# GDN's memory on the right, RWKV's first operands beside GDN's last scan, and a second place for inverses

## The chip, the cores and the metric

The kernel runs on one core of a Trainium2 chip. The metric is the device time of one execution in microseconds. Three runs of the kernel before gave 3955.95, 3957.01 and 3962.45 us.

## What is computed

Two blocks follow each other on 1024 tokens of width 1024, in float32. The first has two layers; each does this:

```python
h = rms_norm(x, norm_g[layer])
cols = split_columns(h @ w_in[layer])
y_gdn = gdn_branch(cols, ...)    # gated delta rule, 6 heads, both directions, chunks of 64
y_mla = mla_branch(cols, ...)    # attention, 6 heads, low-rank q and kv, rope
y_rwkv = rwkv7_branch(cols, ...) # RWKV-7 recurrence, 4 heads, both directions
mix = concat([y_gdn, y_mla, y_rwkv]) * silu(cols['gate'])
x = x + mix @ w_out[layer]
```

The second block (a gated convolution and a gated linear recurrence) is not touched by the change. It fills the span from about 2500 us on.

## The kernel before

**Stages of a layer.** `layer` (L1664) runs stage A, the projection `h @ w_in` together with the GDN branch, then stage B, MLA together with RWKV, and then the product with `w_out`. All matmuls with weights are split into high and low parts: `product` (L1039) sends three matmuls for every 128 rows of the sum, each recorded at L1045, 48 for one tile of 128 output columns. The projection has 27 such tiles, in the order of `ORDER`; `job` (L1690) stores each half tile to `proj` in DRAM, and whoever needs it loads it from there. The last eight tiles are the gate.

**GDN.** Heads go in three pairs. `gdn_front` (L217) prepares a pair in five parts between its `yield`s: convolutions of q and k; convolution of v, transposes and the decay matrix; the products within a chunk; an inverse on VectorE (`lane_inverse`, L462) and the loads of q2; and the rest of the inverse with the products that the scan needs. `gdn_scan` (L411) is a chain of 14 steps: eight small matmuls into a PSUM tile `psk` (L440), then an addition on VectorE (L442), on which the next step waits. Among the steps it makes the outputs in `pso` (L428, L430); after them come additions (L447), a norm on ScalarE and a last scaling (L458).

**RWKV.** `rwkv_prep` (L501) and `rwkv_features` (L532) load projected tiles and shift them along the tokens (`load_shifted`, L490: a load into a tile `pad`, then L485 to L487). Units 0 to 3 are two groups of heads in two directions. For each, `rwkv_early` (L547) makes the operands `kb` and `rk` (L572 to L599), then `ga` and `gb` from their products, transposes a part of `ga` into `lan` (L635), and inverts it on POOL with `lane_inverse` into `xl` (L468 on ScalarE, then 60 instructions at L475 and L476). `rwkv_late` (L642) turns `xl` (L690, L692) and makes what the scan needs; `rwkv_scan` (L747) is again a chain of 14 steps.

**MLA.** `mla` (L854) loads its three projected tiles on POOL's queue (L864 to L867), norms them, and goes through 24 blocks of scores, softmax and values; it yields at every matmul.

**What sets the order.** The text of the program gives each instruction its precedence. The planner that lays out the program walks through a simulated time and gives an engine, whenever it is free, the ready instruction that was written first; on the chip every engine then follows that order. Two strings set what is written when:

```python
SEQ_A = "0 T6 0 1 1 T6 1 0 S0 1 1 2 2 2 T5 S1 2 2 S2"
SEQ_B = "F0 V0 E0 E1 F1 L0 S0+L12 V1 S1+E22 E3 L2 S2+L32 O0 S3 O1"
```

In SEQ_A a number is the next part of that pair's `gdn_front`, S is its scan, and T6 writes six tiles of the projection. Four tiles stand ahead of the string, and what is left (six tiles here) is written after it. `paced` (L1091) ties every third matmul of the projection to a no-op on SP's queue, so that other work can get in between. In SEQ_B each word is a part of RWKV (F features, V values, E early, L late, S scan, O finish), and `weave` (L782) writes eight steps of MLA ahead of every step of RWKV.

**Memory.** Pools are stacked from the left end of SBUF or, with `side="right"`, from the right; a tile waits for the tiles whose place it takes. On the left lie, in stage A, the normed input `hh` and `hl` with the projection's weights, and above them GDN's tiles; in stage B RWKV's pools `r` and `s` and MLA's `m` take their places. PSUM has eight banks. Stage A uses pss 1 (scan steps), pso 1 (scan outputs), ps 3 (fronts) and psd 2 (projection); stage B uses mT 2, mS 2, rx 3 and mo 1. RWKV's `xl` and `lan` have one buffer each (`RWKV_BUFS`).

Of the kernel before, what the change touches and what calls it, by code (L numbers as in the profile page):

```python
# [95 lines left out]
class K:  # L96
# [19 lines left out]
    def psum(self, ex, **banks):  # L116

        return [
            ex.enter_context(self.tc.tile_pool(name=self.name(nm), bufs=b, space=PSUM, reuse_waits="tile"))
            for nm, b in banks.items()  # L120
        ]
# [289 lines left out]
def gdn_scan(k, hp, F, prm, y_out):  # L411
# [23 lines left out]
    for s in range(1, NST - 1):  # L435
        psk = k.pss.tile([128, 512], F32, tag="sc", name=n("psk"))
# [12 lines left out]
    for x, sl in zip(y, HALVES):  # L449
        sq = F["free"][1][:, sl]  # L450
        nc.scalar.activation(sq, x, AF.Square)
        ps = k.pss.tile([128, 512], F32, tag="sc", name=n("ps"))
# [9 lines left out]
def lane_inverse(k, eng, pool, lan):  # L462
# [3 lines left out]
    xt = pool.tile([128, 32, 32], F32, tag="xl", name=k.name("xl"))  # L466
# [80 lines left out]
def rwkv_early(k, gi, d, F, prm, P, w2a2, E):  # L547
# [12 lines left out]
    lan = g.tile([64, 32, 32], F32, tag="lan", name=n("lan"))  # L560
# [47 lines left out]


# [6 lines left out]
    for b in range(4):  # L616
# [7 lines left out]
        for z, ps in enumerate(pss):  # L624
# [4 lines left out]
            yield  # L629
    for q in range(2):  # L630
# [8 lines left out]
    E.update(kb=kb, rk=rk, ga=ga, gb=gb, ep=ep, xl=lane_inverse(k, nc.gpsimd, g, lan))  # L639
# [1024 lines left out]
def layer(k, L, xs, x_in, x_out, prm_d, prm_at, w_in, w_out, wuq, wukv, cs, next_g):  # L1664
# [3 lines left out]
    with ExitStack() as lx:  # L1668
# [11 lines left out]
        with ExitStack() as hx:  # L1680
            k.pss, k.pso, k.ps, k.psd = k.psum(hx, pss=1, pso=1, ps=3, psd=2)
            hp_ = hx.enter_context(tc.tile_pool(name=n("h"), bufs=1, reuse_waits="tile"))
            hh = hp_.tile([128, 8, T], F32R, name=n("hh"))
            hl = hp_.tile([128, 8, T], F32R, name=n("hl"))
            xs.split_norm(pf("ng"), lambda i, sl: (hh[:, i, sl], hl[:, i, sl]))
            xs.close()
            with ExitStack() as gx:
                wpool = gx.enter_context(tc.tile_pool(name=n("w"), bufs=1, reuse_waits="tile"))
                k.wp = Tagged(wpool, dict(wr=2, wh=3, wl=3, st=2))

                def job(i):
                    def evac(hf, sl, ps):
                        st = k.wp.tile([128, 512], F32, tag="st", name=n("st"))[:, : sl.stop - sl.start]
                        nc.scalar.activation(st, ps, AF.Silu if i >= TI["gate"] else AF.Copy)
                        nc.scalar.dma_start(proj[i][:, sl], st)
                    return w_in[i], ((lambda j: hh[:, j]), (lambda j: hl[:, j])), evac

                steps = dense_steps(k, map(job, ORDER), wait=True)

                tiles = lambda n: run(itertools.islice(steps, n * 48))  # L1700
                tiles(4)
                steps = paced(k, steps)
                with tc.tile_pool(name=n("g"), bufs=1, reuse_waits="tile") as g:
                    k.g = Tagged(g, GDN_BUFS)
                    decays = []
                    fronts = [gdn_front(k, hp, [proj[1 + 3 * hp + a] for a in range(3)], pf, decays, eg) for hp in range(3)]
                    next(fronts[0])
                    misc, _ = pair_of(k, "misc")
                    nc.sync.dma_start(misc, proj[0])
                    decays.extend(gdn_prep(k, misc, pf, eg))  # L1710
                    next(fronts[0])
                    F = [None] * 3
                    for x in SEQ_A.split():
                        if x[0] == "T":
                            tiles(int(x[1:]))
                        elif x[0] == "S":
                            gdn_scan(k, int(x[1]), F[int(x[1])], pf, ys[int(x[1])])
                        else:
                            F[int(x)] = next(fronts[int(x)])
                    run(steps)  # L1720
        with ExitStack() as px:
            k.mT, k.mS, k.rx, k.mo = k.psum(px, mT=2, mS=2, rx=3, mo=1)

            rp, r2, mp = (px.enter_context(tc.tile_pool(name=n(x), bufs=1, reuse_waits="tile")) for x in ("r", "s", "m"))
            k.g = Tagged(rp, RWKV_BUFS, {x: r2 for x in ("ga", "gb", "vz", "lan", "xl", "lt")})
            k.rm = reset_mask(k, rp, T, 0, CH)
            k.constants(rp, "rw", "rwf", "rwb")
            P = rwkv_prep(k, proj[TI["wdad"]], pf)
            w2a2 = rp.tile([128, 2, 256], F32, name=n("w2a2"))
            nc.sync.dma_start(w2a2.rearrange("p d c -> p (d c)"), prm_d[:, npr:])  # L1730
            steps = mla(k, mp, [proj[0], proj[TI["cq0"]], proj[TI["ckv"]]], pf, wuq, wukv, cs, ys[3:6])
            Fs, Es, yts = {}, {}, {}

            def part(x):
                w, u = x[0], int(x[1])
                gi, d = u // 2, u % 2
                if w == "F":
# [117 lines left out]
```

## Time and profile before

| | |
|---|---|
| median of three runs | 3957.01 us |
| the profiled execution's own time | 3981.41 us |
| its span, first to last instruction | 3979.6 us |
| mean granted TensorE clock | 0.916 |
| TensorE busy | 3454.4 us (87%) |
| VectorE, ScalarE, POOL busy | 59%, 45%, 35% |

Times in the rows are microseconds from the span's start. Engines are PE (TensorE), PEld (its weight loads), DVE (VectorE), ACT (ScalarE), POOL and SP; a q behind a name is the engine's queue. A row of a window gives its borders and its length, then the busy time of PE, PEld, DVE, ACT and POOL with the count of instructions (PE alone where one line is asked for), then the granted clock as a share of full speed, the busy share of the DMA engines and GB/s. A row of a timeline gives start, duration, engine, line, operation, what is written and read, and in brackets the engine's idle time ahead of it with what ended it. A row of a group gives its count, its busy time, the mean of one in ns and the idle time ahead of it. Idle time is a window's length less the busy time.

In layer 0 the third GDN scan runs from 560 to 610 us, the projection ends at about 640, MLA's first instruction is at 610, and stage B ends at about 1200. Layer 1 repeats this some 1280 to 1290 us later.

### The profile page before, as it was taken

The page shows a single profiled execution, that of the slowest core. Times are in us where ns is not written, and L with a number is a line of the kernel's source. Part 1 is how long each engine was busy: PE and PEld are TensorE (multiplying, and loading weights), DVE is VectorE, ACT ScalarE, POOL GpSimd, SP SyncE. Part 2 cuts the span into 40 slices and gives each one's busy share as a digit, 9 for nine tenths or more (in the row PEclk, how much of TensorE's full clock was granted, in tenths as well). Part 3 has the DMA queues.
Part 4 walks back from the last instruction along what each step waited for, and adds up shares of the span by engine and source line. Part 5 has one row for each costly group of instructions (what it writes and reads, how often), then busy time and mean ns, then how long its engine had stood idle before and what let it go on. Part 6 is the DMA issues. An engine that isn't in the chain of part 4 may idle for free. (4 is left out here: it accounts for less than half of the span.)

```text
span 3979.6 us, 72088 instructions
## 1 busy us (share of the span) xinstructions
PE 3454.4 (87%) x30444; PEld 2710.6 (68%) x30444; DVE 2349.3 (59%) x3138; ACT 1780.1 (45%) x2798; POOL 1409.3 (35%) x1389
## 2 busy tenths in 40 slices
PE   5897996797887889899679899779999998999898
PEld 4666673575665666667357576668888877887786
DVE  6675544857653567462575864359998975323223
ACT  5533425454552553343545454344344347555222
POOL 3431311534403343131163440433333545333361
PEclk9998997898998899899779888879999999999899
DMA  3321211000014232121100000411111111111432
GB/s 115 102 67 47 70 55 66 20 7 4 7 53 166 83 98 68 44 84 49 56 19 7 4 7 33 155 65 46 49 54 51 39 56 46 55 56 41 162 110 72
DMA packets 107076, 237.35 MB, mean 60 GB/s; under 512 B 13896, under 2 KB 16328, under 8 KB 106752
## 3 DMA queue, kind: packets, MB, share of 16 engines
q1 hardware_dynamic: 88448, 197.87, 15.3%
q10 hardware_dynamic: 17280, 31.46, 2.1%
q8 instruction: 239, 3.92, 0.4%
q0 software_dynamic: 1024, 3.41, 0.3%
q14 instruction: 85, 0.70, 0.1%
HBM read 164.17 MB, written 62.23 MB: 57 GB/s over the span
## 5 line engine op out<-in xcount | busy, mean ns | idle before, releaser
L1045 PE MATMUL psd<-hh,wh 128*128 128x512 f32 (+2 forms) x2272 | 910.3, 401 | 56.4 <-ACT hh L1002 18.9
L1006 POOL TENSOR_TENSOR wl<-wr,wh 128x512 fp32r<-128x512 f32 x332 | 489.3, 1475 | 1233.2 <-ACT wh L1002 1193.3
L1045 PE MATMUL psd<-hl,wh 128*128 128x512 f32 (+2 forms) x2272 | 864.9, 381 | 26.7 <-DVE hl L1006 21.6
L1045 PE MATMUL psd<-hh,wl 128*128 128x512 f32 (+2 forms) x2272 | 863.8, 380 | 9.3 <-POOL wl L1006 9.3
L1045 PEld LDWEIGHTS psd<-hh,wh 128*128 128x128 f32 x2272 | 441.4, 194 | 148.4 <-ACT hh L1002 22.9
L1045 PEld LDWEIGHTS psd<-hl,wh 128*128 128x128 f32 x2272 | 440.7, 194 | 100.2 <-DVE hl L1006 27.8
L1045 PEld LDWEIGHTS psd<-hh,wl 128*128 128x128 f32 x2272 | 441.3, 194 | 79.9 <-POOL wl L1006 13.1
L1002 ACT ACTIVATE wh<-wr 128x512 fp32r<-128x512 f32 x332 | 208.3, 628 | 574.4 <-PE psd L1045 345.2
L1211 DVE SCALAR_TENSOR_TENSOR co<-pad,cw,co 128x1024 f32<-128x1024 f32 x240 | 368.7, 1536 | 5.8
L929 ACT ACTIVATE ph<-ps 128x512 fp32r<-128x512 f32 x192 | 114.3, 595 | 198.3 <-PE pso L937 191.0
L930 DVE TENSOR_TENSOR pl<-ps,ph 128x512 fp32r<-128x512 f32 x192 | 131.8, 686 | 91.2 <-ACT ph L929 88.5
L975 DVE TENSOR_REDUCE m<-pss 128x1 f32<-128x512 f32 x192 | 130.6, 687 | 80.2 <-PE pss L974 78.6
L1045 PE MATMUL psd<-hi,wh 128*128 128x512 f32 x384 | 149.7, 393 | 11.7 <-ACT wh L1002 11.7
L937 PE MATMUL pso<-pl,v 128*64 128x256 f32 x384 | 111.4, 324 | 51.9 <-DVE pl L930 51.3
L937 PE MATMUL pso<-ph,v 128*128 128x256 f32 x384 | 134.3, 353 | 23.9 <-DVE y L941 17.4
L1045 PE MATMUL psd<-hi,wl 128*128 128x512 f32 x384 | 149.4, 392 | 5.3 <-POOL wl L1006 5.3
L476 POOL TENSOR_TENSOR xl<-xl,lt 64x30 f32<-64x30 f32 (+14 forms) x240 | 146.3, 609 | 18.1
L1045 PE MATMUL psd<-lo,wh 128*128 128x512 f32 x384 | 149.9, 393 | 0.0
L979 ACT ACTIVATE p<-pss,m 128x512 f32<-128x512 f32 x192 | 129.8, 683 | 44.1 <-DVE m L976 38.5
L1045 PE MATMUL psd<-mh,wh 128*128 128x512 f32 x256 | 102.1, 414 | 48.8 <-ACT wh L1002 35.9
L475 POOL TENSOR_TENSOR lt<-lan,xl 64x30 f32<-64x30 f32 (+14 forms) x240 | 134.1, 559 | 17.9
L927 PE MATMUL ps<-cst,p 128*128 128x128 f32 x768 | 137.8, 302 | 1.1 <-ACT p L979 1.1
(486 smaller groups left out, 7415.2 us busy)
## 6 DMA issues: line engine op xcount, KB each, us to landing
wr<-in_w_in SPq DMA_DIRECT2D x252, 256.0 KB, 2.7
proj<-st ACTq DMA_DIRECT2D x108, 256.0 KB, 2.1
pad<-proj SPq DMA_DIRECT2D x32, 512.0 KB, 3.7
wr<-in_w_out SPq DMA_DIRECT2D x48, 256.0 KB, 2.9
y<-yd SPq DMA_DIRECT2D x16, 512.0 KB, 5.4
sg<-proj SPq DMA_DIRECT2D x16, 512.0 KB, 4.4
x<-x SPq DMA_DIRECT2D x16, 512.0 KB, 4.1
eg<-eg SPq DMA_DIRECT2D x24, 256.0 KB, 4.1
```

The source lines that it names most:

```text
L475: eng.tensor_tensor(t, a, b, op=ALU.mult)
L476: eng.tensor_tensor(x[:, j + 1 :, 0:j], x[:, j + 1 :, 0:j], t, op=ALU.subtract)
L927: yield nc.tensor.transpose(ps[:, c : c + 128], p[i][kt // 4][:, (kt % 4) * 128 : (kt % 4) * 128 + 128], k.c("ident"))
L929: nc.scalar.activation(ph, ps, AF.Copy)
L930: nc.vector.tensor_tensor(pl, ps, ph.bitcast(F32), op=ALU.subtract)
L937: yield nc.tensor.matmul(o, lhsT=l, rhs=r[:, c], start=kt + i == 0, stop=kt + i == 8)
L975: nc.vector.reduce_max(m[:, h : h + 1], pss[h], axis=AX.X)
L979: nc.scalar.activation(p[h], pss[h], AF.Exp, bias=m[:, 2:3], scale=SCALE, accum_out=sums[:, t, h : h + 1])
L1002: first = nc.scalar.activation(hi, src, AF.Copy)
L1006: e.tensor_tensor(lo, src, hi.bitcast(F32), op=ALU.subtract)
L1045: yield nc.tensor.matmul(ps, lhsT=w(a)(i), rhs=x[b](i)[:, sl], start=i == 0 and a == b, stop=i == 7 and a == 1)
L1211: eng.scalar_tensor_tensor(out, pad[:, j : j + T], w[:, j : j + 1], out, op0=ALU.mult, op1=ALU.add)
```

## The change

It has five parts.

- GDN's pools, and in stage B the pools `s` and `m`, go to the right end of memory; the projection's pools lie alone on the left, in a stack `hx` of their own that can be closed while GDN is still at work.
- T5 becomes T11: all 27 tiles of the projection are written ahead of the second scan.
- A new word R, ahead of the last part of pair 2's front and of the third scan, closes `hx`, opens RWKV's pool `r` in its place, and writes `rwkv_prep`, F0, V0 and the first three steps of E0. A new `yield` in `rwkv_early` makes the third step end where `kb` and `rk` are done. F0 and V0 leave SEQ_B, and E0 goes on there where R left it.
- The scan steps and the scan's norm use the three banks of `ps` in place of a bank of their own (pss). Then rx 3 fits beside stage A's pools, in psd's two banks and the free one.
- The inverses of the second direction (E1, E3) go into a tile of the tag `ec`, not the one buffer of `xl`; `lan` is allocated later, and the tag `fs` moves to pool `s`, as do the two masks `rwf` and `rwb`.

```diff
-SEQ_A = "0 T6 0 1 1 T6 1 0 S0 1 1 2 2 2 T5 S1 2 2 S2"
-SEQ_B = "F0 V0 E0 E1 F1 L0 S0+L12 V1 S1+E22 E3 L2 S2+L32 O0 S3 O1"
+SEQ_A = "0 T6 0 1 1 T6 1 0 S0 1 1 2 2 2 T11 S1 2 R 2 S2"
+SEQ_B = "E0 E1 F1 L0 S0+L12 V1 S1+E22 E3 L2 S2+L32 O0 S3 O1"
...
-        psk = k.pss.tile([128, 512], F32, tag="sc", name=n("psk"))
+        psk = k.ps.tile([128, 512], F32, tag="mm", name=n("psk"))
...
-    xt = pool.tile([128, 32, 32], F32, tag="xl", name=k.name("xl"))
+    if xt is None:
+        xt = pool.tile([128, 32, 32], F32, tag="xl", name=k.name("xl"))
...
+    yield
 
     ga = g.tile([128, 32, CH], F32, tag="ga", name=n("ga"))
...
-    E.update(kb=kb, rk=rk, ga=ga, gb=gb, ep=ep, xl=lane_inverse(k, nc.gpsimd, g, lan))
+    xl = None
+    if d:
+
+        xl = g.tile([128, NST, CH + 1], F32, tag="ec", name=n("xe")).rearrange("p c i -> p (c i)")[:, :1024]
+        xl = xl.rearrange("p (r c) -> p r c", c=32)
+    E.update(kb=kb, rk=rk, ga=ga, gb=gb, ep=ep, xl=lane_inverse(k, nc.gpsimd, g, lan, xl))
...
+        mx, gx, hx = (lx.enter_context(ExitStack()) for _ in range(3))
+        (k.psd,) = k.psum(hx, psd=2)
...
+        k.pso, k.ps = k.psum(gx, "right", pso=1, ps=3)
...
+        def rwkv_start():
+
+            run(steps)
+            hx.close()
+            (k.rx,) = k.psum(mx, rx=3)
+            rp = mx.enter_context(tc.tile_pool(name=n("r"), bufs=1, reuse_waits="tile"))
+            gdn = k.g
+            k.g = rwkv["g"] = Tagged(rp, RWKV_BUFS, {})
+            k.rm = reset_mask(k, rp, T, 0, CH)
+            rwkv["P"] = rwkv_prep(k, proj[TI["wdad"]], pf)
+            rwkv["w2a2"] = w2a2 = rp.tile([128, 2, 256], F32, name=n("w2a2"))
+            nc.sync.dma_start(w2a2.rearrange("p d c -> p (d c)"), prm_d[:, npr:])
+            for x in ("F0", "V0"):
+                run(part(x))
+            rwkv["E0"] = part("E0")
+            run(itertools.islice(rwkv["E0"], 3))
+            k.g = gdn
...
+        k.g = Tagged(gx.enter_context(tc.tile_pool(name=n("g"), bufs=1, side="right", reuse_waits="tile")), GDN_BUFS)
...
+            elif x[0] == "R":
+                rwkv_start()
...
+        gx.close()
         with ExitStack() as px:
-            k.mT, k.mS, k.rx, k.mo = k.psum(px, mT=2, mS=2, rx=3, mo=1)
+            k.mT, k.mS, k.mo = k.psum(px, "right", mT=2, mS=2, mo=1)
+            r2, mp = (px.enter_context(tc.tile_pool(name=n(x), bufs=1, side="right", reuse_waits="tile")) for x in ("s", "m"))
+            k.g = rwkv["g"]
+            k.g.others.update({x: r2 for x in ("ga", "gb", "vz", "lan", "xl", "lt", "fs")})
+            k.constants(r2, "rw", "rwf", "rwb")
...
-                weave([(int(p[2:] or 1), part(p)) for p in x.split("+")], steps)
+                weave([(int(p[2:] or 1), rwkv.pop(p, None) or part(p)) for p in x.split("+")], steps)
```

## Rows read from the trace of the kernel before

**Rows 1.** The page's first lines: span, and busy time of each engine.

```profile
span 3979.6 us, 72088 instructions
...
PE 3454.4 (87%) x30444; PEld 2710.6 (68%) x30444; DVE 2349.3 (59%) x3138; ACT 1780.1 (45%) x2798; POOL 1409.3 (35%) x1389
```

**Rows 2.** Windows by stage, layer 0; the last is layer 1's.

```profile
560.00:610.00 50.00, 50.00 (x488) 38.03 (x489) 6.79 (x18) 17.99 (x24) 6.01 (x5) 1.00 0.17 60
610.00:640.00 30.00, 23.99 (x74) 14.63 (x72) 8.07 (x14) 19.05 (x24) 13.36 (x24) 0.83 0.33 105
640.00:700.00 60.00, 33.29 (x80) 16.21 (x80) 42.25 (x54) 30.34 (x48) 4.04 (x6) 0.64 0.12 40
700.00:780.00 80.00, 60.14 (x311) 41.25 (x311) 71.27 (x96) 33.57 (x63) 54.65 (x73) 0.82 0.08 22
780.00:940.00 160.00, 153.16 (x1749) 114.79 (x1750) 99.95 (x174) 90.36 (x183) 41.77 (x72) 0.95 0.02 7
940.00:1040.00 100.00, 71.71 (x508) 52.16 (x507) 75.96 (x115) 35.10 (x74) 49.81 (x69) 0.83 0.01 2
1040.00:1160.00 120.00, 116.43 (x1584) 92.63 (x1582) 69.02 (x122) 74.94 (x150) 38.32 (x66) 0.99 0.02 6
1160.00:1200.00 40.00, 26.78 (x248) 18.48 (x246) 17.61 (x38) 16.38 (x24) 1.28 (x5) 0.82 0.35 134
1890.00:2060.00 170.00, 113.61 (x431) 68.98 (x430) 118.32 (x161) 75.28 (x121) 72.64 (x103) 0.74 0.14 43
```

**Rows 3.** The same windows of the projection's line L1045 alone (PE).

```profile
560.00:610.00 50.00, 38.41 (x146) 1.00 0.17 60
610.00:640.00 30.00, 16.02 (x54) 0.83 0.33 105
```

**Rows 4.** Timeline of VectorE in the third scan, layer 0.

```profile
576.20 0.29 DVE L442 TENSOR_TENSOR kd<-kd,psk 128x128 f32<-128x128 f32 x1 [0.80 <-PE psk L440]
...
588.35 0.29 DVE L442 TENSOR_TENSOR kd<-kd,psk 128x128 f32<-128x128 f32 x1 [1.90 <-PE psk L440]
...
608.55 0.75 DVE L458 SCALAR_TENSOR_TENSOR gk<-gk,prm,gk 128x512 f32<-128x512 f32 x1 [4.44 <-ACT gk L457]
```

**Rows 5.** Groups of VectorE by line from 640 to 700 us: busy, mean ns.

```profile
L487 DVE SCALAR_TENSOR_TENSOR f<-pad,prm,f 128x1024 f32<-128x1024 f32 x3 | 3.8, 1277 | 0.0
...
L574 DVE TENSOR_TENSOR_SCAN cum<-rm,lw 128x1024 f32<-128x1024 bf16 x1 | 2.3, 2291 | 0.0
L485 DVE TENSOR_SCALAR f<-pad,rwc 128x1024 f32<-128x1024 f32 x3 | 2.2, 745 | 0.0
...
L596 DVE TENSOR_TENSOR kms<-ta,f 128x1024 f32<-128x1024 f32 x1 | 1.2, 1226 | 0.0
```

**Rows 6.** Timelines of VectorE and ScalarE around the inverses of E0 and E3, layer 0.

```profile
769.13 1.97 DVE L690 STREAM_TRANSPOSE ga<-xl 32x1024 f32<-32x1024 f32 x1 [1.62 <-POOL xl L476]
...
1030.91 4.12 DVE L635 STREAM_TRANSPOSE lan<-ga 32x1024 f32<-32x1024 f32 x2
...
1054.83 1.06 ACT L468 ACTIVATE xl<-lan 64x1024 f32<-64x1024 f32 x1 [1.05 <-PE ps L705]
...
1092.71 2.01 DVE L690 STREAM_TRANSPOSE ga<-xl 32x1024 f32<-32x1024 f32 x1 [0.89 <-POOL xl L476]
```

**Rows 7.** Timelines of SP's queue and POOL after the third scan, layer 0.

```profile
637.69 0.42 SPq L495 DMA_DIRECT2D pad<-proj  x1
...
638.63 25.71 SPq L495 DMA_DIRECT2D pad<-proj  x3
...
610.40 0.69 POOL L864 DMA_DIRECT2D mc<-cs  x1
```

**Rows 8.** Waits from 640 to 780 us: total, times, longest us.

```profile
POOL ep L588 <- ACT ec L581: 19.8, 1, 19.8
```

**Rows 9.** Timelines: MLA's last copy, RWKV's last store, layer 0.

```profile
1178.57 0.59 ACT L940 ACTIVATE y<-pso 64x512 f32<-64x512 f32 x1 [1.38 <-PE pso L937]
...
1198.96 0.33 SPq L807 DMA_DIRECT2D yd<-ys  x1
```

More of the change, by code (lines that the diff above doesn't have):

```diff
@@ L114, in constants, with psum @@
         self.csts[part] = (t, a)
-    def psum(self, ex, **banks):
+    def psum(self, ex, side="left", **banks):
         return [
-            ex.enter_context(self.tc.tile_pool(name=self.name(nm), bufs=b, space=PSUM, reuse_waits="tile"))
+            ex.enter_context(self.tc.tile_pool(name=self.name(nm), bufs=b, side=side, space=PSUM, reuse_waits="tile"))
             for nm, b in banks.items()
@@ L451, in gdn_scan @@
         nc.scalar.activation(sq, x, AF.Square)
-        ps = k.pss.tile([128, 512], F32, tag="sc", name=n("ps"))
+        ps = k.ps.tile([128, 512], F32, tag="mm", name=n("ps"))
         nc.tensor.matmul(ps, lhsT=k.c("bones"), rhs=sq, start=True, stop=True)
@@ L1679, in layer @@
         eg = dp.tile([12, T], F32, name=n("eg"))
[L1680 to L1684, printed above, removed]
+        mx, gx, hx = (lx.enter_context(ExitStack()) for _ in range(3))
+        (k.psd,) = k.psum(hx, psd=2)
+        hp_ = hx.enter_context(tc.tile_pool(name=n("h"), bufs=1, reuse_waits="tile"))
@@ L1685, in layer @@
+        hh = hp_.tile([128, 8, T], F32R, name=n("hh"))
+        hl = hp_.tile([128, 8, T], F32R, name=n("hl"))
+        with ExitStack() as nx:
+            (k.ps,) = k.psum(nx, "right", ps=3)
             xs.split_norm(pf("ng"), lambda i, sl: (hh[:, i, sl], hl[:, i, sl]))
             xs.close()
[L1687 to L1720, printed above, removed]
@@ new lines, in layer, with part @@
+        Fs, Es, yts = {}, {}, {}
+        rwkv = {}
+        def part(x):
+            w, u = x[0], int(x[1])
+            gi, d = u // 2, u % 2
+            P, w2a2 = rwkv["P"], rwkv["w2a2"]
+            if w == "F":
+                Fs[u] = rwkv_features(k, u, [proj[TI["rw"] + 3 * u + a] for a in range(3)], pf, P)
+            elif w == "V":
+                Fs[u]["v"] = load_shifted(k, proj[TI["rw"] + 3 * u + 2], pf, 3 + 3 * u, P["c0"], "f4")
+            elif w == "E":
+                Es[u] = {}
+                yield from rwkv_early(k, gi, d, Fs[gi], pf, P, w2a2, Es[u])
+            elif w == "L":
+                yield from rwkv_late(k, d, Fs[gi]["v"], Es[u])
+            elif w == "S":
+                if d == 0:
+                    yts[gi] = k.g.tile([128, T], F32, tag="f4", name=n("ys"))
+                yield from rwkv_scan(k, d, Es[u], yts[gi])
+            elif w == "O":
+                rwkv_finish(k, u, Fs[u], pf, P, yts[u], ys[6 + u])
@@ new lines, in layer @@
+        steps = dense_steps(k, map(job, ORDER), wait=True)
+        tiles = lambda n: run(itertools.islice(steps, n * 48))
+        tiles(4)
+        steps = paced(k, steps)
+        k.g = Tagged(gx.enter_context(tc.tile_pool(name=n("g"), bufs=1, side="right", reuse_waits="tile")), GDN_BUFS)
+        decays = []
+        fronts = [gdn_front(k, hp, [proj[1 + 3 * hp + a] for a in range(3)], pf, decays, eg) for hp in range(3)]
+        next(fronts[0])
+        misc, _ = pair_of(k, "misc")
+        nc.sync.dma_start(misc, proj[0])
```

49 lines of the change are left out of this document (21 added, 28 removed).

## The prediction

> **What bounds the kernel now.** I read the page first. The span is 3979.6 us and TensorE is busy for 87% of it, more than any other engine [rows 1]. An average says nothing of one stage, so next come the windows that cut layer 0 at its stage borders [rows 2]. In them the reader is to see three things.
>
> First, the third GDN scan (560 to 610 us) leaves TensorE no idle time: 50.00 of 50.00 us. It is not the scan that fills it. 38.41 us of that are the projection's matmuls and 16.02 us more of them follow after the scan, from 610 to 640 [rows 3]. The projection's last tiles are what the scan hides under, or the other way round.
>
> Second, the stage that follows starts badly. TensorE idles 60.00 - 33.29 = 26.7 us from 640 to 700 and 80.00 - 60.14 = 19.9 us from 700 to 780, 46.6 us together, and VectorE is the full engine there: 42.25 of 60 us, then 71.27 of 80 [rows 2]. Layer 1 does the same: 56.4 us idle of 170.00 in its counterpart of 610 to 780, where layer 0 has 52.6 [rows 2].
>
> Third, from 780 to 1160 TensorE is full again but for a hole from 940 to 1040 (28.3 us idle) [rows 2]. So a layer's time is its TensorE work plus its idle stretches, and a change that only moves work is worth the idle time that it closes less that which it opens.
>
> **The change, part by part** (times of layer 0, each counted twice for the two layers).
>
> *Projection put ahead of the third scan (T5 becomes T11).* Its work is the same; its place in the written order, which is the planner's order of precedence, is now ahead of the second scan. The 16.02 us that ran after the scan [rows 3] run before or among it, so the scan ends up to 16 us later, about 626 instead of 609.3. What the scan hid under is then gone. Its chain is 14 steps; with the projection between them VectorE waits 1.90 us for a step, once without it 0.80 us [rows 4]. Fourteen steps of 0.29 + 0.80 are 15.3 us, and from the last step to the last scaling at 609.3 there are another 21 us [rows 4], so the scan uncovered lasts some 36 us. TensorE has 50.00 - 38.41 = 11.6 us of work for it, which leaves 24.7 us idle. Before, the idle time up to 640 was 6.0 us [rows 2]. Bounds of the new idle time: 6.0 (the planner still weaves the two) and 24.7 (the projection is all done before). I take 20, nearer the second, since the projection now has precedence: **+14 us**.
>
> *RWKV's first operands moved beside that scan (R).* VectorE has for it four shifted loads of 0.75 + 1.28 + 1.28 us, one more product of 1.3, a running sum of 2.3, six products of about 1.2 and two scalings of about 0.75 [rows 5]: 13.2 + 1.3 + 2.3 + 7.2 + 1.5 = 25.5 us. They lie now in the stretch where VectorE is full; beside the scan VectorE is busy for 6.79 us of 50 [rows 2], and that is the cover. If the cover were gone (the scan over before R begins) they would cost what they cost now. Bounds of the gain: 25.5 (each us of VectorE there is a us of idle TensorE) and 0. I take the whole, because VectorE's 71.27 of 80 us says that it is what the stage waits for: **-25.5 us**. What is late next is E0's inverse on POOL: L0's first transpose waited for it at 769.13 [rows 6].
>
> *What R issues besides.* Five loads and some dozen small memsets pass to SP's queue and POOL ahead of the scan's end. One of the pad loads kept SP's queue for 25.71 us, as its buffer had to come free [rows 7]; behind it wait now the masks and MLA's first weights, which are needed only once MLA's norms are done, so I cost this at nothing; uncovered it is at most 25.7. On POOL the copy into ep waited 19.8 us for ScalarE [rows 8]; if it stands ahead of MLA's loads (now at 610.40 [rows 7]) these wait as well. That belongs to the slower rival.
>
> *MLA.* Two of its pools of PSUM banks take over those of the scan's outputs and steps (pso, ps), which are in use to the scan's end, and its SBUF lies where GDN's does. So MLA starts with the scan's end as before, only that this end is later; its 24.0 - 16.0 = 8 us of TensorE work that ran beside the projection's end run beside R's end and E0's second half instead. Four rounds of eight MLA steps less stand ahead of E1. I cost both at nothing within the 20 us above.
>
> *A second place for the inverses.* E3's operand was ready at 1030.91 + 4.12 = 1035.0, its inverse began at 1054.83 behind a TensorE reader of the old one, and L3 waited for it at 1092.71 [rows 6]: 19.8 us of lead. But TensorE idles only 3.6 us from 1040 to 1160 [rows 2], so it can give 0 to 3.6. I take 2: **-2 us**. (E1's inverse falls in a full stretch: nothing.)
>
> *Scan steps in the shared banks.* The steps lose their own bank (pss) and share three with the fronts. No row shows a wait for a bank. Bounds: 0, and 14 steps by one step's shortest wait, 0.80 us [rows 4], 11 us. I take **+1**, since the fronts beside the first two scans run under the projection. Pools at the other end of memory move no instruction: nothing.
>
> *Sum.* +14 - 25.5 - 2 + 1 = -12.5 us a layer, -25 for both. The profiled execution took 3981.4 us (its span and 1.8 us around it), 0.6% above the median of the runs, 3957.0. 3981.4 - 25 = 3956.4, which is 3932 on the median's scale.
>
> **The rivals.**
>
> *A: the scan's stretch falls to the lower clock, and the idle time only moves.* In the rows the granted clock is 1.00 while the scan lies under the projection and 0.64 from 640 to 700, where TensorE is busy 33.29 of 60 us [rows 2]; so there it spent much of the time at the lower of its two levels. With the projection gone from beneath, the scan's 11.6 us at half speed are 23.2, that is +11.6 a layer: -0.9 a layer, -2 in all, **3955**, no change. For it: the scan would be as sparse as that stretch. Against: most of it is latency, and projection may still lie among it. By the Trainium skill, TensorE: Matmul & The Clock Gate, section HAM oscillation, a matmul stream broken by waits falls back to the slow clock and pays for it at each burst, which speaks for this rival.
>
> *B: the RWKV chain is the bound, not TensorE.* Then what counts is when its links start: R's loads at 637.69 [rows 7] go out when the projection ends, 0 to 30 us earlier, say 15; E3's inverse starts 19.8 earlier and L3 with it. -35 a layer, -70 in all: 3911, on the median's scale **3888**. For it: L0 and L3 each waited for POOL's inverse [rows 6]. Against: TensorE's 153 of 160 and 116 of 120 us [rows 2]. [...]
>
> *C: slower, because MLA starts late and its chain ends the layer.* MLA began at 610.40 [rows 7]. If R, which is written ahead of the last front part and the third scan, also takes precedence on VectorE, the scan ends at 609.3 + 16 + 25.5 = 651, and MLA's loads behind it: 40 us late. MLA's last copy is at 1178.57 and the layer's last store at 1198.96 [rows 9], so 20.4 us of that are slack; beyond, each us is paid. +20 a layer, +40: 4021, on the median's scale **3997**. It decides once MLA is late by more than 20 us and does not make it up. For it: nothing but R then covers MLA's norms and first scores. Against: in the starting stage MLA shared VectorE with R's 25.5 us, which are now out of its way.
>
> That the change does nothing at all is not open: the order of issue differs.
>
> **How the numbers follow.** Under 0.2% (8 us) a measurement of this kernel cannot tell from no change. Forecast, -12.5 a layer with its terms off by some 5 each: 3905 to 3948, chance 0.47. A: 0.16. B: 0.13. C, in full or by half: 0.24. So faster 0.47 + 0.13 = 0.60, same 0.16, slower 0.24. The range leaves out the far end of B and the last of C: 3885 to 3988. By the terms' bounds alone it would run from 6.0 - 6.0 - 25.5 - 3.6 = -29 to +18.7 + 0 + 0 + 11 = +30 a layer.
>
> **What would show it.** In the changed profile: no L1045 matmuls beside most of the third scan, its steps nearer 1.1 us than 2.2; R's shifted loads on VectorE before the scan's last scaling; the first 140 us after MLA's start with under 25 us of TensorE idle; E3's inverse started straight after its transposes. It is wrong if the stretch from the last projection matmul to MLA's first scores has more idle time than the start of the stage has lost (A, C), if MLA's last copy comes after the last RWKV store (C), or if TensorE is less than full from 780 to 940 while the layer is much shorter (B).

## The result, and the profile after

The changed kernel takes 3996.24 us (median of four runs, 3991.61 to 4002.63); the kernel before, beside it, 3959.73 us (four runs). The ratio is 1.0089, 95% interval 1.0061 to 1.0116: 35 us slower, where 25 us faster was forecast. The time lies above the range, and on rival C's 3997.

The profiled execution of after took 4002.63 us, its span is 4000.7 us. Its lines carry numbers one to eight higher than those of before (L442 is L443, L864 is L872). The windows of layer 0, with the columns of [rows 2]; the last is the whole stretch from the first GDN scan to the layer's last store:

```profile
560.00:634.00 74.00, 61.75 (x934) 44.70 (x936) 30.77 (x32) 26.95 (x42) 9.54 (x21) 0.78 0.17 57
634.00:672.00 38.00, 28.69 (x363) 23.41 (x362) 7.55 (x21) 10.92 (x13) 5.35 (x8) 0.50 0.13 44
672.00:730.00 58.00, 41.43 (x121) 20.24 (x122) 47.00 (x61) 28.79 (x39) 45.46 (x48) 0.60 0.10 34
730.00:780.00 50.00, 42.68 (x373) 31.09 (x375) 29.54 (x43) 26.64 (x46) 35.59 (x61) 0.76 0.01 1
780.00:940.00 160.00, 148.28 (x1495) 109.01 (x1493) 97.82 (x170) 81.31 (x168) 25.05 (x42) 0.90 0.02 6
...
332.00:1222.00 890.00, 777.00 (x8272) 568.77 (x8272) 502.81 (x809) 416.64 (x723) 268.35 (x367) 0.87 0.11 35
```

The same stretch of before, from the windows of that kernel:

```profile
332.00:1200.00 868.00, 729.86 (x8250) 542.89 (x8250) 501.95 (x806) 414.31 (x720) 266.87 (x367) 0.89 0.11 36
```

TensorE's idle time fell as forecast, from 868.00 - 729.86 = 138 us to 890.00 - 777.00 = 113 us. Its busy time rose by 47 us for about the same count of matmuls, and the layer became 22 us longer. The granted clock of the stretch went from 0.89 to 0.87, so more of it ran at the lower of the two levels; that this alone makes the 47 us is not shown. The profiled execution of before took 3981.41 us, more than all four timed ones, so the growth of the layers in these two traces (22 us here, 8 us in layer 1) adds up to less than the 35 us of the medians.

Now the steps. VectorE's timeline of after, R's shifts and the third scan:

```profile
595.45 0.92 DVE L487 TENSOR_SCALAR wa<-pad,rwc 128x1024 f32<-128x1024 f32 x1 [34.66 <-DMA pad<-proj]
...
640.03 0.29 DVE L443 TENSOR_TENSOR kd<-kd,psk 128x128 f32<-128x128 f32 x1 [0.79 <-PE psk L441]
641.11 0.29 DVE L443 TENSOR_TENSOR kd<-kd,psk 128x128 f32<-128x128 f32 x1 [0.79 <-PE psk L441]
...
670.33 0.75 DVE L459 SCALAR_TENSOR_TENSOR gk<-gk,prm,gk 128x512 f32<-128x512 f32 x1 [3.28 <-ACT gk L458]
```

The scan's steps are down to 0.29 + 0.79 = 1.08 us where nothing else runs, against 0.29 + 1.90 before [rows 4], and R's shifts begin at 595. But the last scaling is at 670.33, where before had 608.55 [rows 4]. POOL's timeline of after shows one who waited for the scan:

```profile
623.72 1.26 POOL L589 COPY ep<-ec 128x15 f32<-128x15 f32 x1 [18.27 <-ACT ec L582]
...
626.68 0.69 POOL L872 DMA_DIRECT2D mc<-cs  x1 [0.38 <-issue]
...
660.28 0.56 POOL L874 DMA_DIRECT2D cq<-proj  x1 [32.39 <-PE pso L431]
```

MLA's load of cq waited 32.39 us for the scan's last output matmuls, since it takes the place of memory that they read. The copy into ep stands ahead of MLA's loads here, and mc goes out 16 us later than in [rows 7], but cq waited for the scan longer than that. In before cq went out right behind mc, as POOL's timeline of before has it:

```profile
611.59 0.56 POOL L866 DMA_DIRECT2D cq<-proj  x1
```

MLA's first scores, on TensorE, in before and then in after:

```profile
655.82 0.79 PE L974 MATMUL pss<-kh,qh 128*128 128x512 f32 x1 [2.21 <-ACT qh L1002]
```

```profile
729.23 0.50 PE L982 MATMUL pss<-kh,qh 128*128 128x512 f32 x1
```

They come 73 us later. What was to come earlier did: the inverses of E0 and E3 and the transposes of L0 and L3. Here they are, with the ends behind them (ScalarE's, VectorE's and SP's timelines of after):

```profile
686.22 1.04 ACT L470 ACTIVATE xl<-lan 64x1024 f32<-64x1024 f32 x1
...
752.41 1.89 DVE L698 STREAM_TRANSPOSE ga<-xl 32x1024 f32<-32x1024 f32 x1
...
1036.43 1.06 ACT L470 ACTIVATE xe<-lan 64x1024 f32<-64x1024 f32 x1 [0.38 <-DVE lan L638]
...
1086.44 4.10 DVE L698 STREAM_TRANSPOSE ga<-xe 32x1024 f32<-32x1024 f32 x2
...
1211.92 0.59 ACT L948 ACTIVATE y<-pso 64x512 f32<-64x512 f32 x1
...
1221.41 0.33 SPq L815 DMA_DIRECT2D yd<-ys  x1
```

L0's transposes are 17 us earlier than in [rows 6], E3's inverse 18, L3's transposes 6. MLA's last copy is 33 us later than in [rows 9] and the last store 22 us. The layer still ends with RWKV: its last store comes 9.5 us behind MLA's last copy, where before had 20.4. From L3's first transposes to that store it took 106 us in before and takes 135 here, so RWKV's lead was lost late in the layer. Its steps there are written interleaved with MLA's, which were late; that this is what held them, no run shows.

### The profile page after: what moved, and what is told of

It reads as the page before. It is cut to its first block, busy times and chain, and to the rows that moved or that the text cites. A ratio compares the mean times of both kernels' runs of the same rounds, so it can differ in the third digit from the quotient of the medians.

```text
span 4000.7 us, 72076 instructions
## 1 busy us (share of the span) xinstructions
PE 3522.7 (88%) x30444; PEld 2739.3 (68%) x30444; DVE 2352.2 (59%) x3138; ACT 1787.6 (45%) x2802; POOL 1414.2 (35%) x1389
## 5 line engine op out<-in xcount | busy, mean ns | idle before, releaser
L1053 PE MATMUL psd<-hh,wh 128*128 128x512 f32 (+2 forms) x2272 | 921.2, 406 | 49.7 <-ACT pad L1442 16.8
L857 POOL TENSOR_TENSOR rt<-rt,mc 32x512 f32<-32x512 f32 x28 | 37.9, 1352 | 310.4 <-DVE rt L855 292.7
L1704 ACT ACTIVATE st<-psd 128x512 f32<-128x512 f32 x108 | 64.3, 595 | 162.6 <-PE psd L1053 161.8
```

The lines of the kernel that those rows point to most:

```text
L857: nc.gpsimd.tensor_tensor(t[96:128], t[96:128], cs[96:128, sl], op=ALU.mult)
L1053: yield nc.tensor.matmul(ps, lhsT=w(a)(i), rhs=x[b](i)[:, sl], start=i == 0 and a == b, stop=i == 7 and a == 1)
```

## The experiments

Each was timed beside the kernel before; a ratio is against that kernel, with its interval, and 0.001 is 4 us. "Kernel 2" is the kernel of run 2, and so on. "Scan end" is the end of the third scan's last scaling in layer 0 (609.3 in before, 671.1 in after).

**1. T11 alone (b_t11).** The kernel before with

```diff
-... 2 2 2 T5 S1 2 2 S2
+... 2 2 2 T11 S1 2 2 S2
```

> The kernel before with T5 changed to T11 and nothing else. Theory P (precedence: the projection's last six tiles, written ahead of the second scan, displace the second scan, the last front part and the third scan, MLA starts late and its chain ends the layer): the second scan runs at about 480 to 535 in layer 0 and not at 411 to 470, the third scan's last scaling comes at 655 to 675 and not at 609, MLA's first scores after 700, and the time is 20 to 50 us above the kernel before, since RWKV's early work fills the same hole here too. Rival Q (the shared banks of the scan steps delay everything): the second scan stays within 15 us of 411 and the time within 10 us of the kernel before. Rival K (only the lower clock beside the uncovered third scan costs): the third scan is uncovered here as well, so +20 to +40 us, with TensorE's busy time from 600 to 780 up by over 25 us.

Measured: 1.0085 (1.0069 to 1.0101), 34 us slower; scan end 654.4, first scores 703.1. The second scan stayed at 408 to 466. So the loss is there with T11 alone, but not through the second scan, where theory P saw it. Rival K falls by its own sign: TensorE's busy time from 600 to 780 rose by 7 us (127.43 to 134.72), not by over 25. VectorE's timeline of the last front part, pair 2, in before and then in this kernel:

```profile
549.09 0.69 DVE L396 TENSOR_TENSOR am<-am,ps 128x512 f32<-128x512 f32 x1 [19.32 <-PE ps L395]
550.95 0.69 DVE L396 TENSOR_TENSOR am<-am,ps 128x512 f32<-128x512 f32 x1 [1.18 <-PE ps L395]
552.85 0.69 DVE L396 TENSOR_TENSOR am<-am,ps 128x512 f32<-128x512 f32 x1 [1.21 <-PE ps L395]
554.69 0.69 DVE L396 TENSOR_TENSOR am<-am,ps 128x512 f32<-128x512 f32 x1 [1.15 <-PE ps L395]
```

```profile
580.28 0.69 DVE L396 TENSOR_TENSOR am<-am,ps 128x512 f32<-128x512 f32 x1 [53.77 <-PE ps L395]
587.31 0.69 DVE L396 TENSOR_TENSOR am<-am,ps 128x512 f32<-128x512 f32 x1 [6.33 <-PE ps L395]
595.42 0.69 DVE L396 TENSOR_TENSOR am<-am,ps 128x512 f32<-128x512 f32 x1 [7.43 <-PE ps L395]
```

The part starts 31 us later, and each of its steps waits over 6 us for TensorE instead of 1.2: the projection, now written ahead, gets TensorE first. The four additions take 22 us from first to last (580.28 to 602.44), where before had 5.6.

**2. The shared banks alone (b_psk).** The kernel before with

```diff
-psk = k.pss.tile(... tag="sc" ...)
+psk = k.ps.tile(... tag="mm" ...)
-k.pss, k.pso, k.ps, k.psd = k.psum(hx, pss=1, pso=1, ps=3, psd=2)
+k.pso, k.ps, k.psd = k.psum(hx, pso=1, ps=3, psd=2)
```

and the same for the scan's norm.

> The kernel before with the scan steps and the scan's norm in the three banks that the fronts use, and nothing else. Theory P: the first scan lasts some 10 us longer (27 us in place of 17), as the changed kernel showed, but the projection covers it; the time stays within 8 us of the kernel before. Rival Q: +20 to +40 us, with the first scan's delay passed on to the second scan (411 becomes 425 or later) and to the layer's end. Rival K: no change.

Measured: 0.9934 (0.9920 to 0.9948), 3928.38 us, 26 us **faster**, which no theory had. It beats both kernels. The windows from 332 to 400 us, in before and then in this kernel:

```profile
332.00:400.00 68.00, 47.63 (x1298) 42.84 (x1300) 23.80 (x36) 29.00 (x39) 9.19 (x10) 0.80 0.16 45
```

```profile
332.00:400.00 68.00, 64.55 (x1243) 52.33 (x1241) 23.12 (x34) 30.94 (x45) 16.21 (x15) 0.97 0.24 76
```

Before had a hole of 20.4 us of idle TensorE, in which 6 matmuls of the projection ran; now 108 do. SP's queue, again before and then this kernel:

```profile
293.70 35.02 SPq L1018 DMA_DIRECT2D wr<-in_w_in  x4
355.21 3.31 SPq L332 DMA_DIRECT2D q<-q  x4
363.39 48.16 SPq L228 DMA_DIRECT2D pad<-proj  x3
412.20 0.33 SPq L1018 DMA_DIRECT2D wr<-in_w_in  x1
```

```profile
291.46 71.58 SPq L1018 DMA_DIRECT2D wr<-in_w_in  x7
363.66 3.19 SPq L332 DMA_DIRECT2D q<-q  x4
370.85 3.50 SPq L228 DMA_DIRECT2D pad<-proj  x2
382.24 11.87 SPq L1018 DMA_DIRECT2D wr<-in_w_in  x2
```

In before four weight loads (wr) stand ahead of pair 2's loads and none goes out between 329 and 412 us; here seven stand ahead. The second scan did move, to 474 to 510: its banks come behind pair 2's third part, and it is shorter (36 us, not 59). So it is the banks, not T11, that displace it.

**3. The changed kernel with the steps' own bank again (a_pss).** The edit of 2 undone.

> The changed kernel with a bank of their own again for the scan steps and the scan's norm, and nothing else. Theory P: the second scan stays at about 475 to 535 and MLA's first scores after 700; the time is 0 to 12 us below the changed kernel, still above the kernel before. Rival Q: the time falls by 30 us or more, to that of the kernel before or below. Rival K: within 8 us of the changed kernel.

Measured: 1.0145 (1.0123 to 1.0167), 22 us above the changed kernel. All three theories missed; it agrees with 2 in sign and size.

**4. Six tiles back behind the second scan (a_t5t6).** The changed kernel with

```diff
-... 2 2 2 T11 S1 2 R 2 S2
+... 2 2 2 T5 S1 2 T6 R 2 S2
```

> The changed kernel with six tiles of the projection put back behind the second scan and pair 2's fourth part (T5 S1 2 T6 R 2 S2), and nothing else. Theory P: the second scan is back at about 415 to 475, the last front part and the third scan move earlier by 20 to 50 us but stay behind those six tiles, MLA's first scores come at 680 to 710, and the time falls by 15 to 35 us from the changed kernel, to about the kernel before. Rival Q: within 8 us of the changed kernel. Rival K: the third scan is still uncovered, so it stays within 10 us of the changed kernel although the scans are earlier.

Measured: 1.0091 (1.0076 to 1.0105), as the changed kernel; scan end 665.2. The second scan ran at 474 to 510 (482 to 535 in after), not at the 415 that theory P asked for, the third scan ended 6 us earlier, and nothing was won. What stayed is that all of the projection and R are written ahead of the last front part and the third scan. That became theory R of the next runs.

**5. R behind the third scan (a_rlast).** The changed kernel with `T5 S1 2 2 S2 R`.

> The changed kernel with R put behind the third scan and T5 in place of T11 (T5 S1 2 2 S2 R): R then has RWKV's old place in the written order, and what is left of the change is the shared banks, the pools on the right and the second place for the inverses. Theory R (R and the projection's last six tiles, which R needs ahead of it, take precedence over the last front part and the third scan, so MLA starts late): the third scan's last scaling is back at about 613 us in layer 0, MLA's first scores at about 665, and the time 60 to 75 us below the changed kernel, within 10 us of the 3928 that the shared banks alone gave. Rival M (the pools on the right or the second place for the inverses cost the time): it stays above 3960. Rival T (T11 alone costs it): also about 3928 here, told apart by the next two runs.

Measured: 1.0000 (0.9986 to 1.0013), 35 us below the changed kernel; scan end 616.7. Theory R has its direction, but 26 us to kernel 2 are missing.

**6. The same with T11 (a_t11_rlast).** `T11 S1 2 2 S2 R`.

> The changed kernel with R put behind the third scan, T11 kept (T11 S1 2 2 S2 R). Theory R, whose first half is that the projection is spent ahead of the last front part and the third scan: about half of the loss comes back, 3950 to 3975, the third scan ending some 20 to 40 us later than 613. Rival T (T11 is the whole of it): it stays at 3985 to 4000. If only R's own instructions cost, then 3925 to 3940.

Measured: 1.0050 (1.0033 to 1.0068); scan end 656.1. T11 costs 20 us here, and R's early place in the text another 15. ScalarE's timeline has E0's inverse in this kernel at

```profile
670.90 1.04 ACT L470 ACTIVATE xl<-lan 64x1024 f32<-64x1024 f32 x1
```

15 us earlier than in after, though R is written last. R's first shift runs at 586 here and at 595 in after, in both ahead of the third scan: its place in the text did not hold it back.

**7. Shared banks and T11 (b_psk_t11).** Kernel 2 with T11.

> The kernel before with the shared banks and T11, nothing else (pools, inverses and RWKV as before). Theory R: like the changed kernel with R last and T11, 3950 to 3975, 25 to 45 us above the shared banks alone, as T11 cost the kernel before 30 us. Rival M: clearly below that run, by over 10 us, since it has neither the pools on the right nor the second place.

Measured: 1.0010 (0.9996 to 1.0024); scan end 630.6. T11 costs 30 us here too, and the rest of the change (right-hand pools, second place, fewer rounds of MLA) 16 us up to kernel 6, as rival M had it.

**8. Two tiles ahead of pair 2's front (b_t2).** The kernel before with `S0 1 1 T2 2 2 2 T3 S1 2 2 S2`.

> The kernel before with two of the five tiles of T5 written ahead of pair 2's first part (S0 1 1 T2 2 2 2 T3 S1 2 2 S2), banks as before. Theory H (the shared banks gain because the projection's weight loads then stand ahead of pair 2's pad loads in the queue of SP, so that the projection runs on from 355 to 412 us, where it stood still at 774 matmuls): the hole closes here too, some 850 matmuls of the projection are done by 400, the projection ends before 620 in layer 0, and the time falls by 15 to 30 us below the kernel before. Rival B (the banks themselves are what gains, as three banks shorten the second scan from 59 to 36 us): the second scan still takes about 59 us and the time stays within 8 us of the kernel before.

Measured: 1.0004 (0.9991 to 1.0017). The hole did not close (8 matmuls of the projection from 332 to 400), so the run does not decide what closing it is worth.

**9. Pad loads on POOL's queue (b_padq).** The kernel before with

```diff
-nc.sync.dma_start(pad[:, 2 : T + 2], raw[i])
+nc.gpsimd.dma_start(pad[:, 2 : T + 2], raw[i])
```

> The kernel before with the fronts' pad loads issued from POOL's queue and not SP's, banks as before and nothing else. Theory H (in the kernel before SP's queue has pair 2's loads ahead of the projection's pace no-ops and weight loads, so the projection stands still at 774 matmuls from 355 to 406 us; the shared banks gain because they change that order): over 830 matmuls of the projection are done by 400 us and the time falls by 10 to 30 us below the kernel before. Rival B (the banks themselves gain, through the second scan): the projection may run on, but the time stays within 8 us of the kernel before.

Measured: 0.9973 (0.9962 to 0.9984), 11 us faster, but again with the hole open (6 matmuls). So the pad loads in SP's queue alone are not what holds the projection there.

**10. 32 steps of MLA ahead of E0, R last (a_rlast_m32).** Kernel 5 with

```diff
+run(itertools.islice(steps, 32))
 for x in SEQ_B.split():
```

> The changed kernel with R behind the third scan and T5 (it took 3959, against 3928 for the shared banks alone), and 32 steps of MLA written ahead of E0, in place of the four rounds that left the interleaving with F0, V0 and the first half of E0. Theory W (those 30 us are MLA's: with four rounds less ahead of it MLA's first block ends 33 us later, 765 and not 732): MLA's first copy is back before 740 and the time within 10 us of 3928. Rival I (they come from the second place for the inverses or from the pools on the right): it stays at 3950 or above.

Measured: 0.9980 (0.9967 to 0.9992), 8 us below 5; MLA's first copy is at 771.87, not before 740. Theory W falls.

**11. Shared banks and the second place (b_psk_inv).** Kernel 2 with the `xe` tile and the later `lan`.

> The kernel before with the shared banks and the second place for the inverses (with lan allocated later), nothing else. My prediction costed that place at -2 us a layer, -4 in all: 3924 by it, within 8 us of the 3928 of the shared banks alone by theory W. By rival I, where it takes precedence from MLA as E3 comes sooner: 3940 or above.

Measured: 0.9979 (0.9966 to 0.9992), 18 us above kernel 2, though E3's inverse starts at 1007 and not at 1036. Rival I's number came out; that E3's early start is the reason is not shown.

**12. The 32 steps in the changed kernel (a_m32).** The edit of 10.

> The changed kernel with 32 steps of MLA written ahead of E0 and nothing else. Theory W: what the four rounds are worth comes back here too, 10 to 30 us below the changed kernel, 3966 to 3986; still above the kernel before, as the projection is still spent ahead of the third scan. Rival I: within 8 us of the changed kernel. If MLA's start at the scan's end, not its precedence, is what holds it, also within 8 us.

Measured: 1.0120 (1.0101 to 1.0139). Scan end 654.4 and first scores 713, both 16 to 17 us earlier than in after, and no gain. So an earlier end of the scan and an earlier start of MLA do not by themselves shorten this kernel.

**13. One place in the changed kernel (a_inv1).** `if d:` became `if False:`.

> The changed kernel with all inverses in the one buffer again, nothing else. Theory I (the second place costs by itself, as E3's inverse and L3 come earlier and take TensorE from MLA): 10 to 20 us below the changed kernel, 3976 to 3986. Rival: it costs only where the rest is undisturbed, so within 8 us of the changed kernel.

Measured: 1.0101 (1.0085 to 1.0117). What cost 18 us in 11 costs nothing here. Here, too, the scan ends 14 us earlier than in after (656.8) without a gain. E3's inverse starts at 1038, with one buffer, against 1036 in after: so little of its lead is the second place's.

**14. Extra matmuls beside the third scan (a_fill).** The changed kernel with, behind the step's own matmuls,

```diff
+if hp == 2 and s > 1:
+    for j in range(4):
+        nc.tensor.matmul(k.fill[:, j * 128 : j * 128 + 128], lhsT=k.c("bones"), rhs=x..., start=True, stop=True)
```

> The changed kernel with four extra matmuls of 128 columns into a spare PSUM bank beside each step of the third scan but the first (52 a layer; their results are not used). Theory K (the uncovered scan lets the clock fall, and what follows runs at the lower level): the granted clock from 634 to 780 us rises from 0.50 to 0.70 to above 0.75, TensorE's busy time without the extra matmuls falls by over 15 us a layer, and the time is 10 to 40 us below the changed kernel. Theory R (only the late end of the third scan counts): the scan ends no earlier, by up to 10 us later, and the time is 0 to 20 us above the changed kernel.

Measured: 1.0115 (1.0097 to 1.0133). The windows of this kernel, against those of after above:

```profile
634.00:672.00 38.00, 32.64 (x418) 26.77 (x416) 5.29 (x14) 8.40 (x10) 4.71 (x6) 0.77 0.12 40
672.00:730.00 58.00, 34.05 (x103) 15.71 (x105) 47.76 (x59) 30.66 (x40) 42.49 (x44) 0.68 0.12 36
730.00:780.00 50.00, 38.01 (x312) 29.45 (x312) 31.46 (x48) 24.61 (x43) 37.92 (x64) 0.78 0.00 1
```

The granted clock beside the scan rose from 0.50 to 0.77, and from 672 to 730 from 0.60 to 0.68. The last two rows cannot be set against after's in busy time, as 415 matmuls ran in them and 494 in after. The layer can; here are its row of this kernel and the extra matmuls by themselves (PE and PEld):

```profile
332.00:1220.00 888.00, 771.45 (x8306) 569.73 (x8302) 496.94 (x802) 415.21 (x720) 273.31 (x367) 0.89 0.11 35
```

```profile
600.00:700.00 100.00, 18.72 (x104) 15.83 (x104) 0.72 0.10 32
```

Without the extra matmuls TensorE was busy for 771.45 - 18.72 = 752.7 us, 24 us less than in after, as theory K asked, and the time did not fall: TensorE only idled longer. The extra matmuls had a price of their own, a scan end 3.7 us and first scores 6 us later, which may hide a gain of that size; the 10 to 40 us of theory K are not there.

**15. Shared banks and pad loads on POOL's queue (b_psk_padq).** The edits of 2 and 9.

> The kernel before with the shared banks and the pad loads on POOL's queue. If the two gains (26 to 30 and 11 us) come from different places they add: 3912 to 3922. If both come from the same place (SP's queue ahead of pair 2's front), then 3922 to 3934.

Measured: 1.0010 (0.9996 to 1.0025), 30 us **above** kernel 2. Neither reading holds: two edits that each won win nothing together.

**16. Shared banks and T3 (b_psk_t3).** Kernel 2 with T3 in place of T5.

> The kernel before with the shared banks and T3 in place of T5, so that two tiles more of the projection come behind the second and third scans. Theory R (each tile of the projection spent ahead of the scans uncovers them; T11, six tiles more, cost 30 to 34 us, so some 5 us a tile): 5 to 15 us below the shared banks alone, 3913 to 3923. Rival: T5 was already enough cover, so within 8 us of 3928 or above it, as the projection then ends later and RWKV's first loads with it.

Measured: 0.9973 (0.9962 to 0.9984), 15 us above kernel 2; scan end 614.9 against 613.7. T5 was cover enough; why T3 costs 15 us is open.

**17. MLA's pool over other tiles (a_swap).** The changed kernel with the pools opened in the order `("m", "s")`.

> The changed kernel with MLA's pool m opened ahead of RWKV's pool s on the right, so that each lies over other tiles of GDN, nothing else. Theory C1 (MLA's wait for the third scan's memory is what the late scan costs): if cq's load comes 15 us or more earlier than 660, MLA's first scores come 15 us or more earlier than 729, and the time is 10 to 30 us below the changed kernel. Theory C2 (the scan's end holds the layer by more than this one wait, by ga, gb and VectorE too): within 8 us of the changed kernel although the load is earlier. If the load stays at 655 to 665, the run says nothing.

Measured: 1.0082 (1.0068 to 1.0095). POOL's timeline:

```profile
647.33 0.56 POOL L874 DMA_DIRECT2D cq<-proj  x1 [26.76 <-PE psk L441]
```

The load is 13 us earlier, a little short of what C1 asked for, the first scores 8 us, the time the same. As far as it goes, that speaks against C1. C2 gets little from it, for the scan's end came 7 us earlier too (663.8), and that won nothing either.

**18. T4 in the kernel before (b_t4).**

> The kernel before with T4 in place of T5, nothing else. Theory S (an edit that hardly changes the stages re-sorts the planner's order enough to move the time by up to 16 us either way): between 3940 and 3975, the third scan's end within 12 us of 609. Theory R alone (each tile ahead of the scans costs some 5 us): 3950 to 3954, hardly to be told from no change. Above 3975 or below 3940 neither holds.

Measured: 0.9998 (0.9988 to 1.0007). No change, and no sign of a spread from this neighbour.

**All of them together.** Ten kernels end the third scan between 603.9 and 619.5 us (before and runs 2, 5, 8 to 11, 15, 16, 18): their ratios are 0.9934 to 1.0010. Run 7 ends it at 630.6: 1.0010. Nine end it between 654.4 and 674.8 (after and runs 1, 3, 4, 6, 12 to 14, 17): 1.0050 to 1.0145. No kernel of one group lies within the other's range. That ties the loss to what the late group has in common, the whole projection written ahead of the third scan (run 7 has that too), but not to the scan's end itself: within the late group the time does not follow it (656.1 in run 6 with 1.0050, 654.4 in run 12 with 1.0120, 665.2 in run 4 with 1.0091). The edits within a group move the time by up to 30 us in ways that no theory here foresaw. The six early ones that have both shared banks and T5 or T3 (2, 5, 10, 11, 15, 16) have a mean of 0.9979, 8 us below the kernel before. As the other edits in them have effects of their own, this is no measure of the banks, but it shows that run 2's 26 us do not last when something else is edited.

## Why the prediction was wrong

**What bounds the kernel.** The reading of idle stretches stood, and the idle time fell by 25 us in layer 0. The rule drawn from it, that a move is worth the idle time that it closes, did not hold: about the same count of matmuls took 47 us more, and in run 14 24 us less of busy time became idle time and left the whole as it was.

**T11, +14 a layer.** Measured 34 us alone, 30 and 20 in other surroundings (runs 1, 7, 6): 10 to 17 a layer, within the bounds, but by another way. The step "the scan ends up to 16 us later, about 626" was wrong: it ended at 654 with T11 alone and at 671 in after. I counted only the 16 us of matmuls that had run behind the scan; but precedence over the last front part makes each step of that part wait (run 1), and the scan starts behind it.

**R, -25.5 a layer.** This is the step that failed: -51 us for both layers were forecast, and R's early place cost 15 (run 6 against after). The work did go beside the scan, whose uncovered length was some 37 us as forecast, and VectorE's busy time in the stretch behind it fell (42.25 + 71.27 of 140 us in [rows 2], 47.00 + 29.54 of 108 in after). But the layer got longer: "VectorE's 71.27 of 80 us says that it is what the stage waits for" took a full engine for the path. E0's inverse, at 686.22 in after, came 30 us earlier than in ScalarE's timeline of before:

```profile
716.25 1.06 ACT L468 ACTIVATE xl<-lan 64x1024 f32<-64x1024 f32 x1 [2.18 <-DVE lan L635]
```

Even that need not be R's doing: kernel 2, without R, has it at 680.34, and kernel 6, with R last, at 670.90. What R's early place does show is that it gets between the operations of the last front part (L397), as VectorE's timeline of after has it:

```profile
602.18 0.68 DVE L397 TENSOR_TENSOR am<-am,ps 128x512 f32<-128x512 f32 x1
...
606.37 0.68 DVE L397 TENSOR_TENSOR am<-am,ps 128x512 f32<-128x512 f32 x1
...
615.80 0.75 DVE L487 TENSOR_SCALAR f<-pad,rwc 128x1024 f32<-128x1024 f32 x1
616.46 0.68 DVE L397 TENSOR_TENSOR am<-am,ps 128x512 f32<-128x512 f32 x1
...
622.38 0.66 DVE L397 TENSOR_TENSOR am<-am,ps 128x512 f32<-128x512 f32 x1
```

The four take 20.2 us from first to last here and about 8 in kernel 6, where R is last; there R's work lies among the scan's steps instead, which last 33 us and not 21. From the first of the four to the scan's end it is 69 us in after and 63 in kernel 6. So R's precedence explains some 6 of the 15 us by which the scan ends later; the other 9 lie ahead of that part. And the scan's end does not explain the 15 us of the whole: kernels 12 and 13 have R early and the scan's end of kernel 6, and their ratios are 0.005 to 0.007 higher than its.

**What R issues besides, 0.** No run shows this term by itself. The 25.71 us in [rows 7] are a row of three loads together, not of one.

**MLA, 0.** "MLA starts with the scan's end as before" was true of the rule and not of the size: cq's load 49 us later, first scores 73, last copy 33. MLA made up 40 of the 73, and the 20.4 us of slack [rows 9] did not cover the rest. That MLA's late start is what made the layer longer fits these rows, but it is argued: where MLA's first scores came 16 us (run 12) or 8 us (run 17) earlier, nothing was won.

**Second place, -2 a layer.** E3's inverse did start at once, 18 us earlier, for nothing. The place was worth 0 in after (run 13) and cost 18 us in all in kernel 2 (run 11).

**Shared banks, +1 a layer.** Wrong in sign: -26 us alone (run 2), -22 in after (run 3). My lower bound was 0, since no row shows a wait for a bank; but a bank also orders work, and the hole at 355 us, which closed in run 2, lies outside the stretch that I cut into windows.

**The sum.** By runs 2, 7, 6 and after, each against the one ahead: -26 for the banks, +30 for T11, +16 for the rest and +15 for R's early place, 35 us. Forecast for both layers were +2, +28, -4 and -51. T11's size was right, R was off by 66 us, and the errors at the banks and the rest partly cancel. In another order the terms differ, as T11's three sizes show.

**The rivals.** C had the direction and, by luck, the number: 3997 against 3996.24. Its outline is there: MLA late by over 20 us and a scan end at 671 (its sum has 651). Its working is not: T11 alone puts the scan's end 45 us late where C counts 16 for it, R adds less than its 25.5, and C's own sign, MLA's last copy behind RWKV's last store, did not come (1211.92 and 1221.41). I gave it 0.24, since I held MLA's share of VectorE to be freed. A named a real fall, the clock at 0.50 in the scan's stretch, but not the price: run 14 lifted it and won nothing. The Trainium skill, TensorE: Matmul & The Clock Gate, section HAM oscillation, has a stream broken by waits fall back to the slow clock. The 0.50 agrees with it; that the fall costs time here, run 14 does not show. B (whose sum makes 3887, not 3888) falls: L0, E3 and L3 came 6 to 18 us earlier and the layer ended 22 us later. The Trainium skill, Perfetto Trace Analysis, section Identifying the Most-Contended Engine, judges TensorE's headroom by MFU (the share of its peak that the matmuls reach) and by the busy share of its weight loads. From 780 to 940 these took 109.01 of 160 us in after and 114.79 before [rows 2]; no run here shows whether RWKV's chain could have used that room.

**The signs.** The scan's steps near 1.1 us, R's shifts ahead of the scan's last scaling and E3's inverse straight behind its transposes came as forecast. The sign of less than 25 us of idle TensorE in the first 140 us after MLA's start did not: from cq's load at 660.28 it is 140 - 108.27 = 31.7 us.

**What stays open.** What sets the layer's end, if an earlier MLA does not shorten it, is not shown. Nor is why R early costs more than its scan end explains (runs 12, 13 and 17 end the scan at 654 to 664, run 6 at 656, and they are 0.003 to 0.007 slower), nor what puts the neighbours of kernel 2 up to 30 us apart. The pools at the right end, which I priced at nothing, were never run by themselves; they are in the +16 of the sum. What closes the hole at 355 us was not found either: two edits aimed at it left it open.

## What to carry to other kernels

Work that depends on nothing, like a projection's tiles, is the cover that dependent chains run under. Written ahead of them it costs time (T11: 34, 30 and 20 us), for with precedence it delays every step of the chain; once the chains are covered, more of it behind them wins nothing (run 16).

A full engine is not the path because it is full. Before hiding its work, look for an edit that only moves the end of that work, and see whether the stage's end follows: here E0's inverse came 30 us earlier and the layer ended 22 us later. The same holds for a long wait in a trace: MLA's load waited 32 us, and 13 us of that taken away (run 17) won nothing.

An edit that moves a planner's order should be timed with a few neighbours: the mean over run 2 and its five neighbours is 8 us, not run 2's 26.

## What the runs showed that was not expected

- Three shared banks instead of a bank of its own made the second scan shorter (59 to 36 us) and the kernel 26 us faster, although the steps of the first scan became slower (17 to 28 us).
- A granted clock raised from 0.50 to 0.77 over 38 us won no time (run 14).
- Two edits that win 26 and 11 us alone win nothing together (0.9996 to 1.0025).
- Ending the third scan 14 to 17 us earlier in the changed kernel won nothing (runs 12 and 13).
